# Layer 0 of a two-layer encoder trunk projects the input before its norm is known, and scales the results

## The chip, the cores and the metric

The kernel runs on one core of one Trainium2 chip, as one program. The metric is the device time of one execution in microseconds (us), as the median of several executions. The engines are named as the profile names them: PE is TensorE (matrix products; PEld its weight loads), DVE is VectorE, ACT is ScalarE, POOL is GpSimd, SP is the engine that starts most DMAs.

## The reference

One sequence of 256 tokens, model width 2048, two layers, everything in float32. Per layer (`i`), with `_rmsnorm(x, g)` = x / sqrt(mean(x²) + eps) · g:

```python
hn = _rmsnorm(h, norm_g[i])
u = hn @ w_in[i]
a_val, a_glu, a_z, q, k, v, b_z = jnp.split(u, offs, axis=-1)
ya = _conformer_conv(a_val, a_glu, conv_w[i], conv_b[i], cln_g[i], cln_b[i])
ya = ya * jax.nn.silu(a_z)
...
yb = _window_attention(q, k, v, bias_band, sink[i]) * jax.nn.silu(b_z)
h = h + jnp.concatenate([ya, yb], axis=-1) @ w_out[i]
e = _rmsnorm(p[i] @ w_pe[i], pe_g[i])
h = h + e * jax.nn.sigmoid(h @ w_pg[i])
```

`_conformer_conv` is a·sigmoid(glu), a depthwise convolution of 31 taps along the tokens, a LayerNorm over its 1024 channels, and SiLU. The attention has 16 query heads and 4 key heads of 64, a window of 128 tokens, a relative-position bias and a sink logit per head. `p[i]` is a per-layer embedding of width 256. A final RMSNorm closes the trunk. Since the norm's factor is one number per token, hn @ W is the same as ((h · g) @ W) times that factor of the token.

## The kernel before

Everything lies with channels on the 128 partitions and the 256 tokens along the free axis; a product's result, 128 channels by 256 tokens, is half a PSUM bank, and most results are handled as a bank of two (128x512). A float32 operand is written as a rounded high part (a cast on ACT, type fp32r) and a remainder (a subtraction on DVE); a product of two such operands is three products on PE: high by high, high by remainder, remainder by high (`mm3`, L401 to L403).

The weights stream in "halves" of 512 KB, in the order of the list `HALVES`: 156 per layer. A layer takes them so: 4 of w_pe (the embedding's projection, tile `e`), 32 of `ag` (value and gate columns of the convolution group: the first two tiles together, then one by one), 4 of k, 4 of v, 32 of `zb` (the attention's gate) and q alternating, 16 of `za` (the convolution's gate), 32 of w_out (`o`; first all that goes with `yb`, then all that goes with `ya`), 32 of w_pg (`g`). Each half is loaded into `raw` (pairs of halves, three buffers), cast and subtracted into `w` (five buffers; `split`, L168 and L171), so splits run up to four halves ahead of the products. A half holds 24 products, 3 for each of 8 blocks of 128 channels.

In layer 0 before the change, PE begins with the embedding in plain float32 (L487, 64 passes), while x is loaded, its squares are added (ACT and DVE, the last piece at L495), PE sums them over the partitions into a column per token (`rh0c`, L354), POOL takes the power −1/2 (`rh0col`, L361), and PE makes a row of it that stands on all partitions (`rh0b`, L368). Then DVE makes `hn` = x · gain · row (L455), ACT its high part (L458), DVE the remainder (L459), and the first ag product can run.

The order of work on DVE, PE and ACT is the order in which the program is written (the scheduler is switched off for them). After each half, `pump()` moves side work along: it advances every generator in `side` (attention of each pair of heads, bias, the embedding's norm) by one step, and a queue of convolution taps on DVE (L566, 8 tiles of some 30 instructions per layer) by so many taps as `RATES` says per half. At the last pair of za tiles `finish` runs all taps that are left. Then come the LayerNorm's mean on PE (`mean`, L720, it takes the last taps' tiles) and the products with yb, whose remainders DVE makes there (L755). `embed` squares e tile by tile (ACT), adds the squares (`eacc`, on POOL, L392) during the ag and k halves, and makes the row of the embedding's norm. `rstd_row(..., settle=n)` puts 2n single-column products into PE ahead of the row (L370).

Of the kernel before, what the change touches and what calls it, by code (L numbers as in the profile page):

```python
# [56 lines left out]
NWARM = 6  # L57
QQ = ((4, 5), (2, 4))
# [21 lines left out]
def weight_halves():  # L80
# [7 lines left out]
    for q in range(4):  # L88
        out.append(("w_pe", q, 0, 2))
    for ts in FIRST_TILES:  # L90
        for k0 in (0, 8):
            for t in ts:
                for off in (OFF_VAL, OFF_GLU):
                    out.append(("w_in", off + tile_cols(t), k0, 8))
    for t in range(2):
# [24 lines left out]
HALVES = weight_halves()  # L120
NHALF = len(HALVES)
# [8 lines left out]
def trunk_kernel(ctx: ExitStack, tc: tile.TileContext, xT, pT, wst, par, gain, relb, sinkp, onehot, out):  # L130
# [23 lines left out]
    state = {"raw": -1, "spl": 3, "credit": 0.0}  # L154
    raws, spl = {}, {}
# [7 lines left out]
    def split(h):  # L163
        raw = raws[h // 2][:, h % 2, :]
        w = wspl.tile([P, 2 * HALF + 64], F32R, tag="w", name=f"w{h}")
        w = w[:, SHIFT:SHIFT + 2 * HALF].rearrange("p (t n) -> p t n", t=2)
        hi, lo = w[:, 0], w[:, 1]
        nc.scalar.copy(hi, raw)  # L168
        spl[h] = w
        if h not in (4, 5):  # L170
            nc.vector.tensor_sub(lo, raw, hi.bitcast(F32))  # L171

    def first_lo(h):

        w = spl[h]
        nc.vector.tensor_sub(w[:, 1], raws[h // 2][:, h % 2, :], w[:, 0].bitcast(F32))

    def ahead(h):

        while state["spl"] < min(h, TOT - 1):  # L180
            n = state["spl"] + 1
            while state["raw"] < min(n // 2 + LD - 1, TOT // 2 - 1):
                state["raw"] += 1
                load(state["raw"])
            if HALVES[n % NHALF][0] != "w_pe" or n >= NHALF:
                split(n)
            state["spl"] = n

    def get(h):

        r = h % NHALF
        if r < 12:
# [8 lines left out]
    RATES = (3.3, 2.6, 3.3)  # L201

    def pump(taps=None):
        taps = RATES[(Cursor.h % NHALF > 4 + 32 + 8 + 12) + (Cursor.h % NHALF > 4 + 32 + 8 + 32 + 4)] if taps is None else taps
# [58 lines left out]
    def load_p(l):  # L263
        pf = wk.tile([P, 2, S], F32, name=f"p{l}", tag="v", bufs=1)
        (nc.sync if l == 0 else nc.gpsimd).dma_start(pf, pT[l])
        return pf

    def load_half(c, x, eng=nc.sync, n=1):

        if c not in raws:  # L270
            raws[c] = wraw.tile([P, 2, HALF], F32, tag="raw", name=f"raw{c}")
        w = HALF // n
        for i in range(n):
            eng.dma_start(raws[c][:, x, i * w:(i + 1) * w], wst[c, :, x * HALF + i * w:x * HALF + (i + 1) * w])

    def load_x(k, eng=nc.sync):
        eng.dma_start(h[k // 8][:, k % 8:k % 8 + 4, :], xT[:, k:k + 4, :])

    h = halves(bigt("x"))

    load_half(0, 0, nc.scalar, 2)
    pf = load_p(0)
    load_half(0, 1)
    load_x(0, nc.scalar)
    load_x(4)
    load_half(1, 0, nc.scalar)
    load_x(8)
    load_x(12)
    load_half(1, 1)
    load_half(2, 0)  # L290
    gains = cst.tile([P, (DEPTH + 1) * KT], F32, name="gains")
    nc.sync.dma_start(gains, gain)
    load_half(2, 1)
    state["raw"] = 2
    pars = cst.tile([P, DEPTH * PW], F32, name="pars")
    nc.sync.dma_start(pars, par)
# [52 lines left out]
    def rstd_col(parts, dim, name, idles=0):  # L349

        c = bank(name + "c")
        for x, a in enumerate(parts):
# [3 lines left out]
            if x == 0 and idles:  # L356
                idle(idles)
        v = wk.tile([P, 2], F32, name=name + "v", tag="rv")
        nc.vector.tensor_scalar(v, c[:, 0, 0:2], 1.0 / dim, EPS, ALU.mult, ALU.add)
# [79 lines left out]
    for l in range(DEPTH):  # L439

        e = halves(bigt(f"e{l}"))
        eacc = wk.tile([P, 2, S], F32, name="eacc", tag="hacc")
# [26 lines left out]
        def copied(j, b, e=e):  # L469
            nc.scalar.copy(e[j // 8][:, j % 8:j % 8 + 2, :], b)  # L470

        for q in range(4):
            n = Cursor.h
            Cursor.h += 1
            if l:
                w = get(n).rearrange("p t (j k c) -> p t j k c", j=4, k=2)
            else:
                raw = raws[n // 2][:, n % 2, :].rearrange("p (j k c) -> p j k c", j=4, k=2)
            for jj in range(0, 4, 2):
                j = 4 * q + jj  # L480
                b = bank("e")
                for x in range(2):
                    for k in range(2):
                        if l:
                            mm3(b[:, x, :], w[:, :, jj + x, k, :], pp[:, :, k, :], x == 0 and k == 0, k == 1)
                        else:
                            nc.tensor.matmul(b[:, x, :], raw[:, jj + x, k, :], pf[:, k, :], start=x == 0 and k == 0,  # L487
                                             stop=k == 1, skip_group_check=True)
                if l == 0 and j // 2 < 4:
                    for k in (4 * (j // 2), 4 * (j // 2) + 2):  # L490
                        if k < KT - 2:
                            square_acc(hacc, h[k // 8][:, k % 8:k % 8 + 2, :], k == 0, nc.vector)
                    if j // 2 == 3:
                        sq = wk.tile([P, 2, S], F32, name="sq", tag="sq", bufs=3)
                        nc.scalar.activation(sq, h[1][:, 6:8, :], AF.Square)  # L495
                        hparts = halves_of(sq) + [fold(hacc)]
                if j // 2 == QQ[l][0]:
                    dg = rstd_col(hparts, D, f"rh{l}")
                    ahead(5 if l == 0 else Cursor.h - 1 - q + 5)
                if j // 2 == QQ[l][1]:  # L500
                    rbs.append(rstd_row(dg, f"rh{l}", copy=False))
                    if l == 0:
                        first_lo(4)
                        operands(0, 1)
                        first_lo(5)
                        subs.pop(0)()
                        operands(2, 1)
                if QQ[l][1] + (l == 0) <= j // 2 <= QQ[l][1] + 1:
                    operands(4 * (j // 2 - QQ[l][1]), 2)
                ecopy.append((j, b))  # L510

                while ecopy and 4 * (l == 0) <= j // 2 < 6:
                    copied(*ecopy.pop(0))
            pump()
        subs.pop(0)()
        ahead(Cursor.h + 3)
        for c in ecopy:
            copied(*c)
        hsrc = xT if l == 0 else hscr

        def embed(l=l, eacc=eacc, e=e):

            if l == 0:
                yield from wait(4)
                bias_prep()
# [414 lines left out]
```

## Time and profile before

| | us |
|---|---|
| median of 3 runs | 937.57 (937.34 to 937.88) |
| profiled execution | 938.7 |
| its span | 936.9 |
| PE busy | 923.9 (99%) |
| DVE busy | 767.6 (82%) |
| ACT busy | 549.2 (59%) |
| POOL busy | 82.0 (9%) |

The span is the time from the first to the last instruction of the profiled execution; 1.8 us of that execution lie outside it. Busy times of an engine count its instructions, whether or not anything waits for them. PE's ends are modelled, and consecutive products overlap: a row's length of a product (0.28 us) is more than the distance of two starts. In the timeline's rows stand the start, the length, the engine, the line, the operation and its tiles, the shape, the count, and in brackets the idle time before with what ended it. PEclk is the clock that PE was granted, 1.00 or 0.50 of full speed. Line numbers in rows are those of the kernel before.

### The profile page before, as it was taken

How to read it: one execution, taken by the hardware profiler on the slowest of the kernel's cores; microseconds unless marked ns; L12 is line 12 of the kernel's file. 1: busy time of each engine (PE TensorE's matmuls, PEld its weight loads, DVE VectorE, ACT ScalarE, POOL GpSimd, SP SyncE). 2: the span in 40 equal slices, each digit the busy share in tenths (PEclk: the TensorE clock that was granted, in tenths of full speed). 3: DMA queues.
4: the chain of work that ended last, by engine and by line, in shares of the span. 5: the costliest groups of instructions: out<-in, count | busy, mean ns of one | idle time of the engine just before them, and what ended most of it. 6: DMA issues, size and time to landing. Idle time of an engine off the chain costs nothing.

```text
span 936.9 us, 19106 instructions
## 1 busy us (share of the span) xinstructions
PE 923.9 (99%) x7960; PEld 909.7 (97%) x7960; DVE 767.6 (82%) x1282; ACT 549.2 (59%) x830; POOL 82.0 (9%) x79
## 2 busy tenths in 40 slices
PE   8999999999999999999999999999999999999995
PEld 7999999999999999999999999999999999999995
DVE  3999999998887786787679999999888877777663
ACT  4655454878874555554566445568788546445551
POOL 0013001001000000011102100100100000000111
PEclk9999999999999999999999999999999999999999
DMA  7674656555547455546555556565555554654532
GB/s 298 226 250 150 220 180 230 190 196 175 189 171 247 166 209 212 191 181 230 211 189 193 181 212 226 174 213 196 183 169 180 193 197 152 247 183 179 200 114 91
DMA packets 29011, 182.55 MB, mean 195 GB/s; under 512 B 3595, under 2 KB 4156, under 8 KB 9084
## 3 DMA queue, kind: packets, MB, share of 16 engines
q1 hardware_dynamic: 24284, 165.70, 50.1%
q0 software_dynamic: 3344, 12.88, 4.2%
q10 hardware_dynamic: 1296, 2.75, 0.8%
q8 instruction: 62, 1.02, 0.4%
q14 instruction: 25, 0.20, 0.1%
HBM read 177.09 MB, written 4.23 MB: 194 GB/s over the span
## 4 chain that ended last, share of the span: by engine, by line
PE 75%; DVE 19%; ACT 2%; issue 2%; DMA 1%; ACTq 0%; DVEq 0%
DVE cz L566 8%; DVE w L171 8%; PE o L401 6%; PE o L402 6%; PE o L403 6%; PE g L401 6%; PE g L403 6%; PE g L402 6%; PE ag L403 4%; PE ag L401 4%; PE ag L402 4%; PE za L401 3%; PE za L403 3%; PE za L402 3%; PE av L679 2%
## 5 line engine op out<-in xcount | busy, mean ns | idle before, releaser
L171 DVE TENSOR_TENSOR w<-raw,w 128x1024 fp32r<-128x1024 f32 x306 | 375.1, 1234 | 99.5 <-ACT w L168 98.6
L168 ACT CAST w<-raw 128x1024 fp32r<-128x1024 f32 x308 | 315.6, 1046 | 157.8 <-PE ag L403 42.5
L566 DVE SCALAR_TENSOR_TENSOR cz<-az,pars,cz 128x241 f32<-128x241 f32 (+11 forms) x480 | 215.9, 499 | 1.0
L401 PE MATMUL ag<-hg,w 128*128 128x256 f32 x512 | 141.8, 277 | 0.0
L403 PE MATMUL ag<-hg,w 128*128 128x256 f32 x512 | 141.6, 277 | 0.0
L402 PE MATMUL ag<-hg,w 128*128 128x256 f32 x512 | 141.5, 276 | 0.0
L403 PE MATMUL g<-h,w 128*128 128x256 f32 x512 | 141.3, 276 | 0.0
L401 PE MATMUL g<-h,w 128*128 128x256 f32 x512 | 141.3, 276 | 0.0
L402 PE MATMUL g<-h,w 128*128 128x256 f32 x512 | 141.3, 276 | 0.0
L401 PEld LDWEIGHTS ag<-hg,w 128*128 128x128 f32 x512 | 96.1, 188 | 0.9 <-ACT u L575 0.8
L403 PEld LDWEIGHTS ag<-hg,w 128*128 128x128 f32 x512 | 96.2, 188 | 0.1
L402 PEld LDWEIGHTS ag<-hg,w 128*128 128x128 f32 x512 | 96.1, 188 | 0.0
L401 PEld LDWEIGHTS g<-h,w 128*128 128x128 f32 x512 | 96.1, 188 | 0.0
L402 PEld LDWEIGHTS g<-h,w 128*128 128x128 f32 x512 | 96.1, 188 | 0.0
L403 PEld LDWEIGHTS g<-h,w 128*128 128x128 f32 x512 | 96.1, 188 | 0.0
L401 PE MATMUL za<-hg,w 128*128 128x256 f32 x256 | 71.7, 280 | 0.0
L401 PE MATMUL o<-yb,w 128*128 128x256 f32 x256 | 71.6, 280 | 0.0
L401 PE MATMUL q<-hg,w 128*128 128x256 f32 x256 | 71.5, 279 | 0.0
L401 PE MATMUL zb<-hg,w 128*128 128x256 f32 x256 | 71.5, 279 | 0.0
L402 PE MATMUL o<-yb,w 128*128 128x256 f32 x256 | 71.0, 277 | 0.0
L402 PE MATMUL q<-hg,w 128*128 128x256 f32 x256 | 71.0, 277 | 0.0
L403 PE MATMUL zb<-hg,w 128*128 128x256 f32 x256 | 71.0, 277 | 0.0
(223 smaller groups left out, 2264.4 us busy)
## 6 DMA issues: line engine op xcount, KB each, us to landing
raw<-in_wst SPq DMA_DIRECT2D x153, 1024.0 KB, 4.9
bias<-fscr POOLq DMA_DIRECT2D x16, 384.0 KB, 3.9
raw<-in_wst SPq DMA_DIRECT2D x4, 512.0 KB, 7.9
az<-in_xT POOLq DMA_DIRECT2D x4, 512.0 KB, 6.0
hscr<-e POOLq DMA_DIRECT2D x2, 1024.0 KB, 5.6
az<-hscr POOLq DMA_DIRECT2D x4, 512.0 KB, 5.4
x<-in_xT SPq DMA_DIRECT2D x3, 512.0 KB, 8.2
out_t<-og ACTq DMA_DIRECT2D x4, 256.0 KB, 3.0
```

Of the source, the lines that this page charges most:

```text
L168: nc.scalar.copy(hi, raw)
L171: nc.vector.tensor_sub(lo, raw, hi.bitcast(F32))
L401: nc.tensor.matmul(o, w[:, 0], x[:, 0], start=start, stop=False, skip_group_check=True)
L402: nc.tensor.matmul(o, w[:, 0], x[:, 1], start=False, stop=False, skip_group_check=True)
L403: nc.tensor.matmul(o, w[:, 1], x[:, 0], start=False, stop=stop, skip_group_check=True)
L566: nc.vector.scalar_tensor_tensor(acc[:, t, lo_:hi_], a[:, t, lo_ + s:hi_ + s], w(k), acc[:, t, lo_:hi_], ALU.mult, ALU.add)
L679: nc.tensor.matmul(o[hh * HD:(hh + 1) * HD, x, :], v[:, kt, g * HD:(g + 1) * HD], pt[hh][:, kt, :], start=x == 0 and kt == 0, stop=kt == 1 ...
```

## The change

In layer 0, x is projected without its norm:

- The operands `hg` are gain · x: the high part is made by ACT directly from x, the remainder by DVE, tile by tile (L563, L564 of the changed kernel). The first two ag tiles (halves 0 to 7 of the list) are computed in four groups of 48 products as quarters of the weights (256 KB) and pieces of x land. w_pe stands behind them in the list, and its products are split too: 96 instead of 64 passes.
- The sum of squares comes from a second copy of x with tokens on partitions (a new input `xtok`, 2 MB in eight DMAs): eight squares on ACT that add along the row. POOL takes the root; the row (`rh0rb`, tile `scaled`) is made on PE ahead of the embedding's third quarter, with two settles.
- Each result of layer 0's projections is scaled by that row on DVE as it leaves PSUM (`evicted`, L599 and L601: 21 instructions of 128x512: 8 of ag, 1 of k, 4 each of q, zb and za); v's scale is part of its copy on ACT. ACT reads the scaled tile one or two pumps later (`DELAY`). The queries come before the gates of their pair. Layer 0's first rate of taps is 3.1 instead of 3.3.
- In both layers the embedding's squares move from the ag stage to the second half of w_out, with the adds on DVE instead of POOL, and its row gets settle=2.
- pars, relt, oh and sinkt are loaded later, seven warm-up passes run instead of six, and p of layer 0 comes behind a memset on DVE.

How PE's order at the start stands before (the names: `e` the embedding's result, `p` its input, `rh0c`, `rh0b` the norm):

```order
L261 MATMUL warm<-zeros 128x256 x6
L487 MATMUL e<-p_90,raw_87 128x256 x16
L487 MATMUL e<-p_90,raw_95 128x256 x4
L354 MATMUL rh0c<-ones,sq 128x1 x4
L354 MATMUL rh0c<-ones,fold 128x1 x2
L487 MATMUL e<-p_90,raw_95 128x256 x4
L368 MATMUL rh0b<-ident,rh0col 128x128 x2
L487 MATMUL e<-p_90,raw_95 128x256 x8
L401 MATMUL ag_0_260<-hg_0_214,w_196 128x256
```

And after, the same place:

```order
L266 MATMUL warm<-zeros 128x256 x7
L449 MATMUL ag_0_151<-hg_0_149,w_155 128x256
L450 MATMUL ag_0_151<-hg_0_149,w_155 128x256
L451 MATMUL ag_0_151<-hg_0_149,w_155 128x256
L449 MATMUL ag_0_151<-hg_0_149,w_155 128x256
L450 MATMUL ag_0_151<-hg_0_149,w_155 128x256
L451 MATMUL ag_0_151<-hg_0_149,w_155 128x256
```

The embedding and the norm's products have left the head of PE's list. What ACT has there after the change, in front of those products (three DMAs of weight quarters, then operands' high parts and quarters' casts):

```order
L285 DMA raw_92<-in_wst 128x512 x2
L285 DMA raw_97<-in_wst 128x512
L302 ACT_TABLE_LOAD
L302 ACTIVATE junk<-zeros 128x1
L563 ACTIVATE hg_0_149<-x,gains 128x256
L179 CAST w_155<-raw_92 128x512
L563 ACTIVATE hg_0_149<-x,gains 128x256 x3
L179 CAST w_164<-raw_92 128x512
L179 CAST w_167<-raw_97 128x512
L179 CAST w_170<-raw_97 128x512
```

One operand and one cast stand before the first product, the other three operands and the other quarters behind them. DVE at the end of layer 0's gates, before (taps `cz`, splits `w`, remainders `yb`):

```order
L566 SCALAR_TENSOR_TENSOR cz_258<-az_257,pars,cz_258 128x243
L566 SCALAR_TENSOR_TENSOR cz_258<-az_257,pars,cz_258 128x242
L171 TENSOR_TENSOR w_3494<-raw_3340,w_3494 128x1024
L566 SCALAR_TENSOR_TENSOR cz_258<-az_257,pars,cz_258 128x241
L171 TENSOR_TENSOR w_3522<-raw_3340,w_3522 128x1024
L755 TENSOR_TENSOR yb_3551<-az_257,yb_3551 128x512 x4
```

And after (`ev<-za_6` is the scaling of the last pair of za tiles, `rh0rb` the row):

```order
L180 TENSOR_TENSOR w_3622<-raw_3436,w_3622 128x1024
L622 SCALAR_TENSOR_TENSOR cz_466<-az_465,pars,cz_466 128x245 x2
L622 SCALAR_TENSOR_TENSOR cz_466<-az_465,pars,cz_466 128x244
L599 TENSOR_TENSOR ev<-za_6_3515,rh0rb 128x512
L622 SCALAR_TENSOR_TENSOR cz_466<-az_465,pars,cz_466 128x244
L622 SCALAR_TENSOR_TENSOR cz_466<-az_465,pars,cz_466 128x243
L622 SCALAR_TENSOR_TENSOR cz_466<-az_465,pars,cz_466 128x242
L622 SCALAR_TENSOR_TENSOR cz_466<-az_465,pars,cz_466 128x241
L622 SCALAR_TENSOR_TENSOR cz_466<-az_465,pars,cz_466 128x243
L622 SCALAR_TENSOR_TENSOR cz_466<-az_465,pars,cz_466 128x242
L622 SCALAR_TENSOR_TENSOR cz_466<-az_465,pars,cz_466 128x241
L904 TENSOR_TENSOR yb_3663<-az_465,yb_3663 128x512 x4
```

The scaling of the last za result now stands in front of seven taps, and those in front of yb's remainders. The core of the diff:

```diff
-NWARM = 6
+NWARM = 7
+DELAY = (1, 0)
+O_LAST = 4 + 32 + 4 + 4 + 32 + 16 + NB_FIRST
...
-        for off in (OFF_BZ, OFF_Q):
+        for off in (OFF_BZ, OFF_Q) if l else (OFF_Q, OFF_BZ):
...
-    RATES = (3.3, 2.6, 3.3)
+    RATES = ((3.1, 2.6, 3.3), (3.3, 2.6, 3.3))
...
+            for n in range(4):
+                c = slice((n % 2) * (HALF // 2), (n % 2 + 1) * (HALF // 2))
+                ks = range(4 * n, 4 * n + 4)
+                def part(k):
+                    i, kk = k // 8, k % 8
+                    hi, lo = (x[:, kk, :] for x in halves(hg[i]))
+                    nc.scalar.activation(hi, h[i][:, kk, :], AF.Copy, scale=gcol(l, k))
+                    nc.vector.scalar_tensor_tensor(lo, h[i][:, kk, :], gcol(l, k), hi.bitcast(F32),
+                                                   ALU.mult, ALU.subtract)
+                for y in range(4):
+                    for k in ks[:1] if y == 0 else ks[1:] if y == 1 else []:
+                        part(k)
+                    split_part(4 * (n // 2) + y, c)
+                if n == 1:
+                    small_loads()
+                for y in range(4):
+                    w = spl[4 * (n // 2) + y].rearrange("p t (k c) -> p t k c", k=8)
+                    for k in ks:
+                        mm3(firsts[y // 2][:, y % 2, :], w[:, :, k % 8, :], hg[k // 8][:, :, k % 8, :],
+                            y % 2 == 0 and k == 0, k == KT - 1)
...
+            hilo(pp[:, 0], pp[:, 1], pf)
+            ahead(9)
+            later_loads()
+            for x, y in enumerate(xts):
+                nc.scalar.activation(y, y, AF.Square, accum_out=xs[:, x // 4, x % 4:x % 4 + 1])
...
+            rcol = root(xs[:, :, 0], D, f"rh{l}")
+
+        def evicted(b, scale=None):
+            if scaled is None:
+                return b
+            u = wk.tile([P, 2, S], F32, name="ev", tag="sq", bufs=3)
+            if scale is None:
+                nc.vector.tensor_mul(u, b, bcast2(scaled))
+            else:
+                nc.vector.scalar_tensor_tensor(u, b, scale, bcast2(scaled), ALU.mult, ALU.mult)
+            return u
...
+                if q == 2:
+                    scaled = rstd_row(rcol, f"rh{l}", settle=2)
...
+            while Cursor.h % NHALF < O_LAST:
+                yield
             for j in range(0, KT, 2):
-                yield from wait(2)
-                square_acc(eacc, e[j // 8][:, j % 8:j % 8 + 2, :], j == 0)
+                square_acc(eacc, e[j // 8][:, j % 8:j % 8 + 2, :], j == 0, nc.vector)
+                yield
...
-            eb = rstd_row(dg, f"re{l}", "reb")
+            eb = rstd_row(dg, f"re{l}", "reb", settle=2)
...
-            b = pair(hg, f"za{l}_{t}")
+            b = evicted(pair(hg, f"za{l}_{t}"))
             if t == NCT - 2:
                 finish(l)
...
-                nc.scalar.copy(v[:, b, :], vb[b][:, 0, :])
+                nc.scalar.activation(v[:, b, :], vb[b][:, 0, :], AF.Copy, scale=rcol[:, b:b + 1])
```

More of the change, by code (lines that the diff above doesn't have):

```diff
@@ L86, in std @@
         out.append((name, cols, 8, 8))
-    for q in range(4):
-        out.append(("w_pe", q, 0, 2))
+    if l:
+        out += W_PE
     for ts in FIRST_TILES:
@@ L129, in trunk_kernel @@
 @with_exitstack
-def trunk_kernel(ctx: ExitStack, tc: tile.TileContext, xT, pT, wst, par, gain, relb, sinkp, onehot, out):
+def trunk_kernel(ctx: ExitStack, tc: tile.TileContext, xT, xtok, pT, wst, par, gain, relb, sinkp, onehot, out):
     nc = tc.nc
@@ L264, in load_p @@
         pf = wk.tile([P, 2, S], F32, name=f"p{l}", tag="v", bufs=1)
-        (nc.sync if l == 0 else nc.gpsimd).dma_start(pf, pT[l])
+        nc.gpsimd.dma_start(pf, pT[l])
         return pf
[L268 to L274, printed above, removed]
@@ new lines, in load_x @@
+    def load_x(k, n=4, eng=nc.sync):
+        eng.dma_start(h[k // 8][:, k % 8:k % 8 + n, :], xT[:, k:k + n, :])
+    h = halves(bigt("x"))
+    gains = cst.tile([P, (DEPTH + 1) * KT], F32, name="gains")
+    pars = cst.tile([P, DEPTH * PW], F32, name="pars")
+    pf = wk.tile([P, 2, S], F32, name="p0", tag="v", bufs=1)
+    load_x(0, 2)
+    load_part(0, 0, nc.scalar)
+    nc.sync.dma_start(gains, gain)
+    load_part(1, 0, nc.scalar)
+    load_x(2, 2)
+    load_part(2, 0, nc.scalar)
+    junk = wk.tile([P, 1], F32, name="junk", tag="junk", bufs=1)
@@ L285, in trunk_kernel @@
+    nc.scalar.activation(junk, zeros[:, 0:1], AF.Copy, scale=2.0)
+    load_part(3, 0)
     load_x(4)
-    load_half(1, 0, nc.scalar)
+    for x in range(4):
+        load_part(x, 1)
     load_x(8)
+    for x in range(4, 8):
+        load_part(x, 0)
     load_x(12)
[L289 to L295, printed above, removed]
@@ L296, in trunk_kernel @@
-    nc.sync.dma_start(pars, par)
+    for x in range(4, 8):
+        load_part(x, 1)
+    xts = []
+    for b in range(2):
+        for c in range(4):
+            if b == 0:
+                y = wk.tile([P, 2, S], F32, name="xt", tag="s", bufs=4)
+            elif c < 2:
+                y = wk.tile([P, 2, S], F32, name="xt", tag="ptt", bufs=2)
+            else:
+                y = wk.tile([P, 2, 3 * P], F32, name="xt", tag="bias", bufs=2)
+            y = y.rearrange("p a b -> p (a b)")[:, 0:2 * S]
+            xts.append(y)
@@ L439, in trunk_kernel @@
     for l in range(DEPTH):
-        e = halves(bigt(f"e{l}"))
-        eacc = wk.tile([P, 2, S], F32, name="eacc", tag="hacc")
+        if l:
+            e = halves(bigt(f"e{l}"))
+            eacc = wk.tile([P, 2, S], F32, name="eacc", tag="hacc")
         hg = []
@@ L467, in trunk_kernel, with copied @@
         ecopy = []
-        def copied(j, b, e=e):
+        def copied(j, b):
             nc.scalar.copy(e[j // 8][:, j % 8:j % 8 + 2, :], b)
[L472 to L475, printed above, removed]
-                w = get(n).rearrange("p t (j k c) -> p t j k c", j=4, k=2)
-            else:
[L478 to L514, printed above, removed]
@@ L897, in pack @@
     for l in range(DEPTH):
[L898 removed]
+        for n, (name, cols, k0, nk) in enumerate(HALVES[l * NHALF:(l + 1) * NHALF]):
             w = W[name][l]
```

256 lines of the change are left out of this document (178 added, 78 removed).

## The prediction

> **What bounds the kernel now.** I read the page first, then what TensorE (PE) waits for, then its timeline where it waits, then windows.
>
> ```profile
> span 936.9 us, 19106 instructions
> PE 923.9 (99%) x7960; PEld 909.7 (97%) x7960; DVE 767.6 (82%) x1282; ACT 549.2 (59%) x830; POOL 82.0 (9%) x79
> ```
>
> PE is busy for 99% of the span. Its list of waits (engine, line, releaser: total us, times, longest) names one that this change touches at the start and one in the attention:
>
> ```profile
> PE rh0c L354 <- ACT sq L495: 1.1, 1, 1.1
> PE sc L636 <- DVE qq L696: 0.6, 2, 0.4
> ```
>
> Time is won only where PE idles or works on something dear. That is the start (start, length, work, count):
>
> ```profile
> 5.57 1.99 PE L487 MATMUL e<-p,raw 128*128 128x256 f32 x8
> 8.03 7.17 PE L487 MATMUL e<-p,raw 128*128 128x256 f32 x32 [0.46 <-DMA raw<-in_wst]
> 16.35 1.05 PE L354 MATMUL rh0c<-ones,sq 128*128 128x1 f32 x8 [1.15 <-ACT sq L495]
> 17.71 3.31 PE L487 MATMUL e<-p,raw 128*128 128x256 f32 x8
> 21.24 3.79 PE L487 MATMUL e<-p,raw 128*128 128x256 f32 x16
> 24.69 0.47 PE L401 MATMUL ag<-hg,w 128*128 128x256 f32 x1
> ...
> 42.01 1.03 PE L329 MATMUL fps<-oh,relt 33*16 33x511 f32 x2
> ```
>
> Until 24.69 us PE has only the embedding's 64 fp32 passes, 0.216 us each (the last 16 from 21.24 to 24.69), so 13.8 us of work in 19.1 us. Windows (start:end and length; busy us and count of PE, PEld, DVE, ACT, POOL; then PEclk, DMA share, GB/s; the first row is of the tile ag alone, without POOL):
>
> ```profile
> 24.66:48.50 23.84, 22.93 (x192) 22.58 (x193) 0.40 (x1) 0.38 (x1) 1.00 0.66 230
> ...
> 14.77:18.18 3.41, 2.26 (x16) 1.84 (x16) 2.17 (x6) 2.54 (x4) 0.05 (x1) 1.00 1.12 395
> 18.18:21.59 3.41, 3.41 (x10) 2.67 (x10) 1.11 (x2) 3.25 (x6) 1.57 (x1) 0.50 0.68 263
> ...
> 50.00:190.00 140.00, 139.72 (x1226) 139.31 (x1225) 137.11 (x242) 79.66 (x116) 18.02 (x14) 1.00 0.58 204
> 290.00:460.00 170.00, 170.00 (x1495) 169.84 (x1494) 123.98 (x147) 86.93 (x107) 10.34 (x10) 1.00 0.57 203
> ```
>
> The first two ag tiles (192 products, with fps's 1.03 among them) end at 48.50: (23.84 - 1.03)/192 = 0.1188 us a product. At 18.18 the clock fell to half for a window. In 50 to 190 PE works for 139.72 of 140, and VectorE (DVE) for 137.11: two engines almost full. From 50 on PE hardly has anything to lose or win, so the sum is made of the start and of waits that the change adds.
>
> **The start.** Before, the end of the first two ag tiles is 48.50. After, the work in that stretch is 192 ag products, 96 split embedding products, fps, and a row. Each term:
>
> Embedding: 64 passes of 0.216 = 13.8 become 96 products. A product in the dense stage costs 139.72/1226 = 0.114 us (products of other kinds are among them), so 10.9; gain 2.9. Idle and half clock in the old start, 24.66 - 5.57 - 13.8 = 5.3 us, go, as no product waits for the root any more. What replaces them is the time until the first split operand:
>
> ```profile
> GB/s 0 16 152 244 266 420 422 418 422 414 422 410 410 401 418 380 389 366 369 410 213 16 0 0 147 188 426 336 205 401 311 82 139 401 401 107 0 33 254 410
> raw<-in_wst ACTq DMA_DIRECT2D x2, 256.0 KB, 5.8
> p<-in_pT SPq DMA_DIRECT2D x1, 256.0 KB, 4.6
> L818 ACT ACTIVATE og<-e,gains 128x256 f32<-128x256 f32 x16 | 7.2, 493 | 0.0
> L458 ACT CAST hg<-hn 128x512 fp32r<-128x512 f32 x16 | 9.9, 621 | 13.7 <-DVE hn L455 13.7
> L455 DVE SCALAR_TENSOR_TENSOR hn<-x,gains,rh0b 128x256 f32<-128x256 f32 x16 | 6.7, 473 | 2.3 <-PE rh0b L368 2.3
> L459 DVE TENSOR_TENSOR hg<-hn,hg 128x512 fp32r<-128x512 f32 x16 | 11.0, 688 | 0.5
> ```
>
> The GB/s row is one figure per microsecond from 0; the others are DMAs (KB, us to land) and groups (mean ns last before the idle time). x's first piece and the first weight quarter stand first in their queues, like p and raw here, and land at the same time, about 5.5 (PE's first pass starts at 5.57). Then ACT makes x's hi (0.49) and casts a quarter (0.62): first product at about 6.65, 1.1 later than now. Per group of 48 products ACT has 4 operands and 4 quarters, 4 x 0.49 + 4 x 0.62 = 4.4; DVE 4 x 0.47 + 4 x 0.69 = 4.6; PE 48 x 0.1188 = 5.7. So once fed, PE paces. The first group is not fed: x's second piece and the second to fourth quarters land by about 8 to 9.3 (the GB/s row sums to 1.5 MB by 7 us, what the group needs, plus landing), and DVE must finish each remainder. I take 1.1 us lost; bounds 0 (each piece lands before its turn) and 2.5 (PE waits for the last piece, then works alone). All four groups need 6.3 MB; the row sums to that by 18, the last group starts after 22. Between the embedding's second and third quarter the root's row (2 small products, 4 of settle) costs 0.7:
>
> ```profile
> 20.82 0.63 PE L368 MATMUL rh0b<-ident,rh0col 128*128 128x128 f32 x2
> L391 ACT ACTIVATE sq<-e 128x512 f32<-128x512 f32 x26 | 16.5, 633 | 18.4 <-DVE e L805 18.4
> 18.13 1.63 POOL L361 TENSOR_TENSOR rh0col<-rh0v,mhalf 128x2 f32<-128x2 f32 x1 [16.81 <-DVE rh0v L359]
> ```
>
> Is the root ready by then? First tiles end at 6.65 + 22.8 + 1.1 = 30.6, the third quarter starts at 36.0. ACT starts its eight squares at about 27.3: ahead of them stands the cast of half 9, into the buffer that half 4's last products leave at 26.3 (5 buffers). 8 x 0.63 = 5.1, two small adds, POOL's 1.63: 34.4. Ready, by 1.6 us; if it were later, each 1 us would cost 1.
>
> So −2.9 − 5.3 + 1.1 + 1.1 + 0.7 = **−5.3 us**: half 12 starts at 43.2, not 48.5.
>
> **A new wait at the end of layer 0's gates.** Here the order of DVE is what counts. Before:
>
> ```profile
> 289.01 0.46 DVE L566 SCALAR_TENSOR_TENSOR cz<-az,pars,cz 128x241 f32<-128x241 f32 x1
> ...
> 291.92 0.28 PE L403 MATMUL za<-hg,w 128*128 128x256 f32 x1
> 292.04 0.59 PE L720 MATMUL mean<-ysum,ones 128*128 128x256 f32 x2
> 292.47 1.03 PE L720 MATMUL mean<-cz,ones 128*128 128x256 f32 x4
> 293.15 0.47 PE L401 MATMUL o<-yb,w 128*128 128x256 f32 x1
> ```
>
> The last tap ended 2.5 us ahead of the last za product; mean follows it without a gap, o starts 1.2 later. After, with 0.2 taps fewer per pump for some 44 pumps, about 9 taps come later: seven stand behind `ev<-za_6`, which waits for that same last product. Behind it on DVE: the scaling (0.60 at pitch, 0.69 alone by the L768 row), seven taps, then yb's remainders, which o needs. From Z, the last product's start: 0.3 for its end, 0.6, seven taps of 0.39 (pitch, from 1.26 for three below) = 2.7: last tap at Z + 3.7, its mean pass until about Z + 4.2, and o behind it. That is **+3.0** against Z + 1.2 (bounds 2.7 and 3.3, by one tap either way). PE idles some 2.8 us of it, in two pieces. Layer 1's order there stays.
>
> **Scalings on DVE.** 21 scalings at the L768 row's pitch, 0.60, are 12.6 us, ten of them in 50 to 190, 6.0 us where DVE has 2.9 free. Against them: 44 x 0.2 taps of 0.39 moved later, 3.4, and POOL's seven adds of squares leave, which slow DVE:
>
> ```profile
> L768 DVE TENSOR_TENSOR az<-o,az 128x512 f32<-128x512 f32 x16 | 10.9, 684 | 0.7 <-PE o L403 0.6
> 77.65 2.23 POOL L392 TENSOR_TENSOR eacc<-eacc,sq 128x512 f32<-128x512 f32 x1 [3.77 <-ACT sq L391]
> 78.65 2.29 DVE L566 SCALAR_TENSOR_TENSOR cz<-az,pars,cz 128x250 f32<-128x250 f32 x3
> 82.00 1.26 DVE L566 SCALAR_TENSOR_TENSOR cz<-az,pars,cz 128x255 f32<-128x255 f32 x3
> ```
>
> Three taps take 2.29 beside a POOL add and 1.26 without: 7 x 1.03 = 7.2 us back. DVE ends lighter by 4.6: the scalings cost 0. The scaled result is read a pump later by ACT, and DVE never waits for ACT there. The same squares now stand in w_out, eight adds of 0.69 on DVE per layer, where DVE has 170 - 124 = 46 us free: 0. There the cover is so large that even doubled they are hidden. xtok's 2 MB go in a stretch (20 to 40) where the GB/s row is mostly below 200: 0. The later loads (pars and the rest) are needed first by the taps and the bias products, after 43: 0.
>
> **Small terms.** Settle: four 128x1 products ahead of a row,
>
> ```profile
> 313.63 0.50 PE L370 MATMUL rv0b<-ones 128*128 128x1 f32 x4
> 314.00 0.36 PE L401 MATMUL o<-yb,w 128*128 128x256 f32 x1
> ```
>
> 0.37 by the distance of the starts, now before two rows more (the embedding's root, both layers): +0.7. The 0.6 us of sc's wait for q's remainders: in layer 0 a whole pair of gates now stands between q and the next q, in both layers DVE is relieved of POOL's adds; I take −0.5, bounds −0.6 and 0. One moved term counts nothing: v is scaled by ACT instead of copied, same length.
>
> **Sum.** −5.3 + 3.0 + 0.7 − 0.5 = −2.1. The profiled execution took 938.7, its span 936.9, the median of the runs 937.57, so it was 1.1 above; after's profile should read 936.6 with a span of 934.8, and the median **935.5**. A difference of 0.2%, 1.9 us (935.7 to 939.4 is "same"), is about what can be told from no change.
>
> **Rivals.**
>
> The finish drops the clock. The 14.77 window above had 12 thin products and four passes, 0.86 of real work, and the next window ran at 0.50, which costs half of 3.41, 1.7 us. In the tail PE kept its clock:
>
> ```profile
> 926.12:929.53 3.41, 1.71 (x13) 1.28 (x12) 2.00 (x5) 0.37 (x1) 1.88 (x2) 1.00 0.15 51
> 929.53:932.95 3.42, 0.00 (x0) 0.00 (x0) 1.90 (x4) 0.00 (x0) 1.32 (x2) 1.00 0.99 361
> 932.95:936.90 3.95, 0.00 (x0) 0.00 (x0) 0.00 (x0) 0.00 (x0) 0.00 (x0) 0.50 0.47 176
> ```
>
> 1.71 of busy time was enough; so the threshold lies between. The finish has 2.8 idle around six mean passes (1.3): a window placed worst holds 0.9 to 1.3 of work. Then 935.5 + 1.7 = 937.2, "same". I give it 0.18.
> The Trainium skill, page "TensorE: Matmul & The Clock Gate", section "Why this matters for your kernels", says a drop needs a gap in the products of over about 3 us. By that rule a gap of 2.8 us in two pieces keeps the clock, this rival has no chance and the sum stays 935.5; the trace doesn't bear it out, since the clock fell after 1.15 us of idle and thin products.
>
> The start is fed late: the bound of 2.5 instead of 1.1 lost, or a window at half clock after the thin warm-up: 935.5 + 1.4 to 1.7, about 937. For it: two engines and two queues must follow each other for the first group; against it: the queues deliver 420 GB/s by 5 us. 0.10.
>
> The start goes better: no loss in the first group (−1.1) and the 192 products at the later 0.114 instead of 0.1188 (−1.0), as no bias products and splits of whole halves stand beside them: 933.4. 0.16.
>
> The other side: the scalings are not covered. If POOL's adds were not what slowed the taps (the three taps beside them may have been slow for ACT's sake), DVE has 6.0 - 2.9 - 3.4 against it, nearly nothing, so this needs more: a scaling waits for its PE result, and all taps and splits behind it wait with it. At 0.6 us of such wait for each of ten, 6 us, PE waits for the remainders: 941.5. It is slower than 939.4 from 3.9 us uncovered. Against it: the splits run up to four halves, 11 us, ahead of PE. 0.08.
>
> **How the numbers follow.** The sum as it stands has 0.48, its own range 934.0 to 936.8 (start 1 us, finish 0.3). Faster: 0.31 of that, and the better start, 0.16: 0.47. Slower: 0.08. Same: the rest, 0.45. The range, 932.8 to 938.3, takes in the better start, the half-clock cases and the sum with all bounds, and leaves out the uncovered scalings and the ends.
>
> **What would show it.** Right: the first product at 6.4 to 7, half 12 near 43.2; a gap of about 2 us on PE behind za_6, put down to DVE cz; no wait of PE for w in 50 to 190; taps without the 2.29 rows there; sc's wait gone. Wrong: PE waits for DVE w in 50 to 190, or PEclk 0.50 behind 285, or half 12 later than 45.

## The result

The changed kernel takes 951.74 us (median of 5, 950.97 to 952.49) against 937.34 before: ratio 1.0152, 95% interval 1.0137 to 1.0167. It is slower by 14.4 us, where 2 us faster was forecast. The profiled execution took 950.98, with this head of its page:

```profile
span 949.2 us, 19291 instructions
PE 933.4 (98%) x7994; PEld 920.2 (97%) x7994; DVE 771.3 (81%) x1322; ACT 558.5 (59%) x861; POOL 58.2 (6%) x65
```

The span grew by 12.3. Marks on PE, read from the two timelines, say where (us; L0 and L1 are layer 0 and 1; "step" is what the difference gained or lost against the mark above):

| mark | before | after | after − before | step |
|---|---|---|---|---|
| third ag tile starts (before: behind fps; after: fps's 0.96 added) | 48.50 | 43.3 | −5.2 | −5.2 |
| L0, last ag product ends | 113.97 | 109.29 | −4.7 | +0.5 |
| L0, last za product ends | 292.20 | 286.37 | −5.8 | −1.1 |
| L0, first o | 293.15 | 291.72 | −1.4 | +4.4 |
| L0, first g | 382.10 | 386.02 | +3.9 | +5.3 |
| L1, last za product ends | 746.04 | 749.85 | +3.8 | −0.1 |
| L1, first g | 836.41 | 845.70 | +9.3 | +5.5 |
| L1, last g ends | 923.62 | 936.31 | +12.7 | +3.4 |
| end of span | 936.9 | 949.2 | +12.3 | −0.4 |

The start gave what it was to give, and a little more followed until the end of the za products: 5.8 us ahead. The four steps of +3.4 to +5.5 behind it lose 18.6. The list of PE's waits names two of their causes:

```profile
PE mean L869 <- DVE cz L622: 3.0, 2, 2.9
PE re1c L398 <- DVE fold L427: 1.9, 1, 1.9
```

**The end of layer 0's gates** (timeline of after, PE, then DVE):

```profile
286.21 0.59 PE L869 MATMUL mean<-ysum,ones 128*128 128x256 f32 x2
289.66 1.22 PE L869 MATMUL mean<-cz,ones 128*128 128x256 f32 x2 [2.86 <-DVE cz L622]
291.06 1.22 PE L869 MATMUL mean<-cz,ones 128*128 128x256 f32 x2 [0.17 <-DVE cz L622]
...
284.73 1.23 DVE L180 TENSOR_TENSOR w<-raw,w 128x1024 fp32r<-128x1024 f32 x1
285.87 1.24 DVE L622 SCALAR_TENSOR_TENSOR cz<-az,pars,cz 128x245 f32<-128x245 f32 x3
287.02 0.69 DVE L599 TENSOR_TENSOR ev<-za,rh0rb 128x512 f32<-128x512 f32 x1
287.62 3.38 DVE L622 SCALAR_TENSOR_TENSOR cz<-az,pars,cz 128x244 f32<-128x244 f32 x7
290.92 2.49 DVE L904 TENSOR_TENSOR yb<-az,yb 128x512 fp32r<-128x512 f32 x4
```

The seven taps stand there as forecast, but the scaling starts at 287.02, 0.6 after za's end: a split and three more late taps are ahead of it. The seven taps also take longer than forecast, 3.30 from the first one's start to that of yb's remainders instead of 2.7: five of them start 0.50 apart, two 0.39. The mean waits 2.86, and its last four passes take 1.22 a pair instead of 0.6.

**The clock** (windows of after: length; busy us and count of PE, PEld, DVE, ACT, POOL; PEclk, DMA share, GB/s):

```profile
285.65:289.07 3.42, 1.15 (x9) 0.75 (x7) 3.35 (x8) 1.33 (x3) 0.00 (x0) 1.00 0.63 184
289.07:292.48 3.41, 2.64 (x6) 1.75 (x7) 3.30 (x8) 1.01 (x3) 0.55 (x1) 0.50 0.29 123
292.48:295.89 3.41, 3.41 (x18) 3.41 (x17) 3.15 (x5) 1.51 (x3) 1.06 (x2) 0.50 0.85 283
821.55:824.96 3.41, 1.67 (x14) 1.70 (x15) 2.19 (x4) 1.18 (x2) 0.00 (x0) 1.00 0.30 58
824.96:828.38 3.42, 3.42 (x18) 3.42 (x17) 3.00 (x5) 1.33 (x2) 1.06 (x1) 0.50 0.59 249
```

Twice a window in which PE was busy for 1.15 and 1.67 of 3.41 us is followed by half clock. The first drop lasts two windows; in the first of these PE was busy for 2.64. All five executions of after have a mean granted clock of 0.992 or 0.993, so these drops are not of the profiled one alone.

**A slow rhythm of PE**, which the prediction did not know. Windows over the 768 products of w_pg (tile g alone, so PE, PEld, ACT), called the last gates in layer 1; first layer 1 before, then both layers after:

```profile
836.41:923.62 87.21, 87.21 (x768) 87.01 (x768) 4.58 (x8) 1.00 0.42 146
```

```profile
386.02:473.22 87.20, 87.20 (x768) 87.00 (x768) 4.58 (x8) 1.00 0.58 206
845.70:936.31 90.61, 90.61 (x768) 90.41 (x768) 4.58 (x8) 1.00 0.40 140
```

The same 768 products, no wait, PEclk 1.00 throughout: 87.2/768 = 0.1135 us each in layer 0 and before, 90.6/768 = 0.1180 in layer 1. From product to product the starts stand 0.1133 or 0.1178 us apart, and one of the two holds for tens of us. Summing what products at 0.1178 take over 0.1133 (without those of the embedding), this rhythm costs 3.4 us in the execution before and 10.2 in the one after: 2.2 in layer 0's w_out, 3.4 in layer 1's g.

So L0's w_out pays about 2.1 for half clock (4.17 us of o until 295.89), 2.1 for slow rhythm (0.1 of it stood there before), 1.4 for the column products and row of the embedding's norm (0.7 each, by the distance of the starts of the o products around them); L1's w_out 1.95 for the wait, 1.6 for half clock, 1.4 for column and row, 0.6 for slow rhythm; L1's g 3.4 for slow rhythm.

### The profile page after: what moved, and what is told of

Its sections match the earlier page's. It is cut to its first block, busy times and chain, and to the rows that moved or that the text cites. A ratio compares the mean times of both kernels' runs of the same rounds, so it can differ in the third digit from the quotient of the medians.

```text
span 949.2 us, 19291 instructions
## 1 busy us (share of the span) xinstructions
PE 933.4 (98%) x7994; PEld 920.2 (97%) x7994; DVE 771.3 (81%) x1322; ACT 558.5 (59%) x861; POOL 58.2 (6%) x65
## 4 chain that ended last, share of the span: by engine, by line
PE 95%; DVE 2%; issue 1%; DMA 1%; ACT 1%; SPq 0%; DVEq 0%; ACTq 0%
PE g L449 6%; PE g L451 6%; PE g L450 6%; PE ag L451 6%; PE ag L450 6%; PE ag L449 6%; PE o L449 6%; PE o L450 6%; PE o L451 6%; PE zb L450 3%; PE zb L449 3%; PE q L450 3%; PE q L449 3%; PE zb L451 3%; PE q L451 3%; PE za L449 3%
## 5 line engine op out<-in xcount | busy, mean ns | idle before, releaser
L180 DVE TENSOR_TENSOR w<-raw,w 128x1024 fp32r<-128x1024 f32 (+1 forms) x316 | 378.5, 1206 | 118.7 <-ACT w L179 117.5
L179 ACT CAST w<-raw 128x1024 fp32r<-128x1024 f32 (+1 forms) x316 | 319.7, 1029 | 175.1 <-PE ag L451 31.1
L622 DVE SCALAR_TENSOR_TENSOR cz<-az,pars,cz 128x241 f32<-128x241 f32 (+14 forms) x480 | 203.5, 476 | 1.2 <-ACT cz L615 0.3
L449 PE MATMUL o<-yb,w 128*128 128x256 f32 x256 | 73.0, 285 | 0.0
L449 PE MATMUL o<-ya,w 128*128 128x256 f32 x256 | 72.3, 283 | 0.0
L450 PE MATMUL o<-yb,w 128*128 128x256 f32 x256 | 72.2, 282 | 0.0
L451 PE MATMUL o<-yb,w 128*128 128x256 f32 x256 | 72.1, 282 | 0.0
L450 PE MATMUL o<-ya,w 128*128 128x256 f32 x256 | 72.0, 281 | 0.0
L451 PE MATMUL o<-ya,w 128*128 128x256 f32 x256 | 71.9, 281 | 0.0
```

The lines of the kernel that those rows point to most:

```text
L449: nc.tensor.matmul(o, w[:, 0], x[:, 0], start=start, stop=False, skip_group_check=True)
L450: nc.tensor.matmul(o, w[:, 0], x[:, 1], start=False, stop=False, skip_group_check=True)
L451: nc.tensor.matmul(o, w[:, 1], x[:, 0], start=False, stop=stop, skip_group_check=True)
L622: nc.vector.scalar_tensor_tensor(acc[:, t, lo_:hi_], a[:, t, lo_ + s:hi_ + s], w(k), acc[:, t, lo_:hi_], ALU.mult, ALU.add)
```

## The experiments

Theories: **A**, late taps and a late fold make PE wait, and the clock drops behind the waits. **B**, DVE simply has no room for the scalings. **C**, an interruption of PE's stream of big products sets its rhythm until the next one. First, A's parts:

```diff
# e1_rate33 (from after)
-    RATES = ((3.1, 2.6, 3.3), (3.3, 2.6, 3.3))
+    RATES = ((3.3, 2.6, 3.3), (3.3, 2.6, 3.3))
# e2_fold3 (from after); e3_both is both
             es = fold(eacc)
-            yield
+            yield from wait(3)
# e4_fill (from after), between mean's ysum pass and its last two tiles
+                if x == 1 and l == 0:
+                    idle(12)
```

> The changed kernel with layer 0's first rate of taps at 3.3 per half, as before the change. Theory A (the loss at the end of layer 0's gates is late taps: seven behind the last scaling and three ahead of it, and two windows at half clock that the idle PE brings): no tap is left behind the last scaling, mean follows za without a long gap, o starts about 1.5 us after the last za product instead of 5.6, no window at half clock there: 951.7 - 4.1 - 2.1 = 945.5; up to 2 less if the slow rhythm of PE in w_out behind it (0.1178 us a product instead of 0.1133) goes too. Theory B (DVE is simply overloaded by the 21 scalings, the rate only moves where it shows): PE waits for DVE w between 50 and 190, by about the same 3 to 4 us, and the time stays within 1 us of 951.7.

946.95 (median of 4, 945.69 to 951.54), ratio to before 1.0115 [1.0088, 1.0142]. No wait but one of 0.3 for yb and no half clock is left at the finish, PE's rows (timeline of e1) are those of before, and o starts 1.0 after za's end:

```profile
287.90 0.59 PE L869 MATMUL mean<-ysum,ones 128*128 128x256 f32 x2
288.33 1.03 PE L869 MATMUL mean<-cz,ones 128*128 128x256 f32 x4
289.01 0.47 PE L449 MATMUL o<-yb,w 128*128 128x256 f32 x1
```

But za now ends at 288.06 instead of 286.37. Its list of waits has a new one:

```profile
PE pt L787 <- ACT s L781: 1.3, 2, 0.9
```

A holds for the finish. B as forecast fell, since the time dropped by 4.8 and PE waits for weights for no more than 0.2, but DVE's load has a share: 1.7 us come back ahead of the finish, 1.3 of them as this wait of the attention.

> The changed kernel with three pumps instead of one between the fold of the embedding's squares and the column products that need it, both layers. Theory A (PE waits 1.9 us for a fold that DVE makes one half of weights too late; idle time and thin products drop the clock for a window): the wait, the window at 825 and so 1.9 + 1.7 us go, 951.7 - 3.6 = 948.1. Theory C (the slow rhythm of PE in the last 100 us, 0.1178 instead of 0.1133, comes from how PE was interrupted there): another 4.0 us go if the rhythm changes with it, 944; if the rhythm is of something else (DVE's or ACT's load), it stays slow and 948.1 holds.

947.12 (943.77 to 947.91), 1.0096 [1.0073, 1.0118]. The wait for the fold is gone, and so is the half clock at 825. The last gates stay slow in the profiled run (90.6 us), so the forecast of 948 holds. 943.77, the lowest of the four, is about what 0.1133 a product there would give; that execution was not profiled.

> Rate 3.3 in layer 0's first stage and three pumps behind the fold together. Theory A: the two add up, 951.7 - 6.2 - 3.6 = 941.9, still over before; with the slow rhythm gone from both w_out stages and the last gates (2.2 + 4.0) 935.7. Theory B: no better than the fold alone, 947 to 948.

943.54 (939.94 to 943.65), 1.0060 [1.0040, 1.0080]: the two nearly add up (−4.8 and −4.6, together −8.2). Three runs lie at 943.5 to 943.65 and one at 939.94; the profile, of that one, has the last gates fast (87.2 us). The mean granted clock of all four is 0.997 or 0.998, so the 3.6 between them is not the clock; it is about what one slow stretch of 768 products costs. The same kernel seems to run either way, though only the one at 939.94 was profiled.

> The changed kernel with twelve products of no use (128x128, some 0.22 us each, 2.6 us in all) on PE between mean's pass over ysum and its passes over the last two tiles, in layer 0: PE is busy while it would wait for the late taps. Theory A: the wait stays, the clock doesn't drop there: 951.7 - 2.1 (o at half clock) - 0.6 (mean's four passes) = 949.0, windows at 285 to 296 all at 1.00. If the clock goes by something else than PE's idle time, 951.7 and windows at 0.50.

948.9 (946.6 to 951.25), 1.0127 [1.0106, 1.0148]. Two windows of it at the bounds of those of after, and the rows of PE:

```profile
285.65:289.07 3.42, 3.42 (x31) 3.37 (x29) 3.31 (x9) 1.54 (x3) 0.00 (x0) 1.00 0.59 213
289.07:292.48 3.41, 2.53 (x15) 1.83 (x15) 3.34 (x7) 1.54 (x4) 0.74 (x2) 1.00 0.22 94
```

```profile
286.43 2.84 PE L391 MATMUL idle<-ident,ones 128*128 128x128 f32 x24
289.46 0.70 PE L871 MATMUL mean<-cz,ones 128*128 128x256 f32 x2 [0.18 <-DVE cz L622]
290.85 0.70 PE L871 MATMUL mean<-cz,ones 128*128 128x256 f32 x2 [0.69 <-DVE cz L622]
```

o starts 0.5 earlier than in after (291.20), so the wait is the taps', but o's first products no longer run at half clock: by the time of the first ya product layer 0 is 2.4 ahead of after. With PE's idle time filled, the clock stayed. The drop at 825 is missing in this profile too, as in that of e1, though both wait 1.9 to 2.0 for the fold like after. In e1 that idle time falls on two windows:

```profile
815.49:818.90 3.41, 2.21 (x20) 2.02 (x18) 3.29 (x4) 1.56 (x3) 0.00 (x0) 1.00 0.42 175
818.90:822.31 3.41, 2.65 (x23) 2.68 (x24) 1.77 (x4) 2.16 (x3) 0.00 (x0) 1.00 0.57 199
```

Neither is as idle as the 1.67 of after, and the clock stays. In e4 the clock's windows lie so that most of the idle time falls in one:

```profile
816.87:820.28 3.41, 1.78 (x16) 1.58 (x14) 3.41 (x5) 1.11 (x2) 0.00 (x0) 1.00 0.25 103
```

PE was busy for 1.78 here, none of it single-column products, and kept its clock; the 1.67 of after has four of those in it (0.58). So whether this wait costs the clock hangs on where it falls in a window. Three of e1's four executions and two of e4's have a mean granted clock of 0.995 where the profiled ones have 0.997; one window more at half clock would make 0.0018, so the drop probably came back in those. The median of e4 is 2.8 lower than after's.

Next, the squares' place, the settle, and the taps:

```diff
# e5_oldemb (from e3): embed of before; squares in ag and k, adds on POOL, row in the attention, no settle
# e6_settle0, e8_settle4 (from e3)
-            eb = rstd_row(dg, f"re{l}", "reb", settle=2)
+            eb = rstd_row(dg, f"re{l}", "reb")            # e8: settle=4
# e7_rates (from e3)
-    RATES = ((3.3, 2.6, 3.3), (3.3, 2.6, 3.3))
+    RATES = ((3.1, 2.9, 3.6), (3.3, 2.6, 3.3))
```

> Rate 3.3 and the embedding's squares, fold, column and row back in the ag and k stages and the attention, adds on POOL, no settle, as before the change (the start unnormed and the scalings stay). Theory C (an interruption of PE's stream sets its rhythm, 0.1133 or 0.1178 us a product, until the next one; the row of the embedding's norm is the last one ahead of 840 products of layer 1): the last one is now the LayerNorm's row, behind which all profiles so far that had no slow w_out before it were fast: the last gates run at 0.1133, 3.4 less than the 943.5 of the version with both repairs, 1.6 less for the column products and rows that leave w_out: 938.5, and up to 1.5 less in layer 0's w_out. Theory B (DVE has no room in ag for scalings beside POOL's adds, so the move of the squares was needed): PE waits for w or for the attention's results by 2 to 7 us more: 941 to 945.

952.03 (948.4 to 956.22), 1.0155 [1.0114, 1.0195], 8.5 worse than e3. Its list of waits:

```profile
PE q L451 <- DVE w L180: 3.8, 2, 3.2
PE pt L788 <- ACT s L782: 2.1, 2, 1.7
```

B is right for this version: with POOL's adds beside the scalings DVE falls behind, PE waits for weights, the clock drops at 141.5, and nearly all later stretches run slow (16 us in the profile). So at these rates of taps moving the squares was needed to pay for the scalings. Those waits are the smaller part, though: of the 15.0 us between the profiled executions of e5 and e3 the slow rhythm makes about 10, and the two waits above 4.6 more than e3's. Theory C's forecast that the last gates would be fast here fell: behind the LayerNorm's row they were slow.

> Both repairs (rate 3.3, three pumps behind the fold), with no settle products ahead of the embedding's row. Theory C (rhythm redrawn by each interruption, its outcome depends on the timing of the pieces): the last gates are fast or slow as a whole, for this kernel mostly one way; 943.5 - 0.7 = 942.8 if slow, 939.4 if fast. Rival (settle products guard against the slow rhythm): slow more often, 942.8 in all runs.

943.47 (942.77 to 947.29), 1.0070. In the profile layer 0's g products are slow (90.6), layer 1's fast: without settle products each layer came out its own way, which neither forecast has.

> Both repairs, but the taps made up for in layer 0's later stages: rates 3.1, 2.9, 3.6 instead of 3.3, 2.6, 3.3. Theory A': with 3.3 in ag and q, DVE fell behind and the transposes waited 1.3 us for ACT at the attention's start, where the changed kernel had no such wait; with 3.1 there and DVE's 10 us of free time from 188 to 284 used for the taps, that wait goes: za ends 1 to 1.7 earlier, 943.5 - 1.3 = 942.2. Rival: the wait comes back in later pairs: 943.5.

938.95 (median of 10), 1.0021 [1.0008, 1.0033]; two of the ten at 942.7, the others at 938.5 to 939.4. The attention's wait is gone and za ends at 286.69. DVE had room for the late taps, in the later stages. The median lies 3.2 under the forecast because the last gates are mostly fast here, by the times of the ten, and were mostly slow in e3; against e3's execution of 939.94 the gain is 1.0.

> Both repairs, with eight single-column products of settle instead of four ahead of the embedding's row. Theory C: the row takes 0.45 longer in each layer, and the rhythm behind it is drawn anew: 944.4 if the last gates are slow, 941.0 if fast. Rival (more settle makes the fast rhythm sure): 941.0 in all runs.

941.52 (940.84 to 943.56), 1.0047. Last gates fast in the profile. Behind the row of layer 1, settle 4 was fast and settle 2 came out either way: more products are no guard by themselves, since in e7, by their times, eight runs of ten are fast with 2.

Then theory C alone, on the kernel before, and a version with all waits repaired:

```diff
# e11_draw2, e12_draw1 (from before), between layer 1's w_out and its gates; 2 or 1
+        if last:
+            for x in range(2):
+                nc.tensor.matmul(bank("draw")[:, 1, 0:1], ones, ones[:, 0:1], start=True, stop=True)
# e9_best (from e7): the last scaling behind yb's remainders; two pumps from fold to column, three to the row
-            b = evicted(pair(hg, f"za{l}_{t}"))
+            b = pair(hg, f"za{l}_{t}")
+            if t < NCT - 2:
+                b = evicted(b)
...
+        begin(rest(evicted(b), 0))
         lgen = lnorm()
# e10_best0: e9 with no settle in the embedding's rows
```

> The kernel before the change, with two single-column products (four passes) between layer 1's w_out and its gates, nothing else. Theory C: an interruption alone redraws the rhythm for the last 768 products: 937.5 + 0.4 = 937.9 in the runs that come out fast, 941.3 in those that come out slow, and at least one of each or all slow. Rival (the slow rhythm comes from the changed kernel's load of DVE or its memory layout, not from the interruption): 937.9 in all runs and pitch 0.1133 in the profile.

> The kernel before the change with one single-column product (two passes) at that place. Theory C: as with two, 937.7 or 941.1. Rival: 937.7 in all runs.

With two products 940.54 (all of six runs 940.3 to 941.9), 1.0036 [1.0022, 1.0049]; with one 937.33 (twelve runs, none over 938.6), 1.0001 [0.9992, 1.0009]. Windows over the g tile of layer 1, of e11 and of e12:

```profile
834.74:925.44 90.70, 90.70 (x768) 90.49 (x768) 4.57 (x8) 1.00 0.40 140
```

```profile
835.14:922.43 87.29, 87.29 (x768) 87.09 (x768) 4.58 (x8) 1.00 0.41 145
```

That is C with nothing else of the change: two products of no use, 0.4 us, put the following 768 into the slow rhythm, 3.4 us; one does not. It isn't drawn by lot here: by their times, all runs with the same count have the rhythm of the one that was profiled. One rival is left in this pair: each of these products takes a PSUM bank of its own, so with two of them the g tiles lie one bank further on than with one. The runs e9 and e14 below settle it: there the extra products share the row's bank.

> The version with the rates 3.1, 2.9, 3.6, and the rest of the losses repaired: the last scaling behind yb's remainders instead of ahead of them (o waits 0.6 less for yb), two pumps between fold and column and three between column and row instead of three and two (the 0.4 to 0.5 that PE waits for POOL's root in layer 1 goes). Theory A: 938.9 - 0.6 - 0.5 = 937.8 with the last gates at the fast rhythm, 941.2 with the slow one. Rival (the waits come back elsewhere): 938.9.

941.24 (six runs, 940.84 to 941.97), 1.0040 [1.0028, 1.0052]: no wait of PE over 0.4 us is left behind the start, but the last gates are slow:

```profile
836.74:927.36 90.62, 90.62 (x768) 90.41 (x768) 4.57 (x8) 1.00 0.41 146
```

> The same without settle in the embedding's rows. Theory C: 937.8 - 0.7 = 937.1 if both stretches of gates are fast, 3.4 more for each that is slow. Rival (the settle products make the fast rhythm likely): slow in one of the two in nearly all runs, 940.5.

944.56 (944.05 to 945.12), 1.0075 [1.0062, 1.0088]: both layers' g products slow. So the count was varied once more, in e9:

```diff
# e13_re1: settle=1; e14_re21: settle=2 - l; e15_re23: settle=2 + l
-            eb = rstd_row(dg, f"re{l}", "reb", settle=2)
+            eb = rstd_row(dg, f"re{l}", "reb", settle=1)
# e16_all1: settle=2 - l there, and
-            rb = rstd_row(dg, f"rv{l}", settle=2)
+            rb = rstd_row(dg, f"rv{l}", settle=1)
```

> The repaired version (941.2) with settle 1 instead of 2 in the embedding's rows of both layers. Theory C (the rhythm behind an interruption depends on how many products it has; one single-column product in the kernel before left it fast, two left it slow): 0.4 less in all, and layer 1's gates fast: 941.2 - 0.4 - 3.4 = 937.4, or 3.4 more if layer 0's gates, fast so far, become slow. Rival (something else of the change costs the 3.9): 940.8.

> The repaired version with settle 2 in layer 0's embedding row (fast behind it so far) and 1 in layer 1's (slow behind 2). Theory C: 941.2 - 0.2 - 3.4 = 937.6. Rival: 941.0.

> The repaired version with settle 2 in layer 0 and 3 in layer 1. Theory C, if an odd number is what matters: 941.2 + 0.2 - 3.4 = 938.0; if only a small number helps: 941.4. Rival: 941.4.

> The repaired version with settle 2 and 1 in the embedding's rows and 1 instead of 2 in the LayerNorm's rows of both layers, behind which layer 0's w_out ran slow (1.4 us). Theory C: 941.2 - 0.2 - 3.4 - 0.4 - 1.4 = 935.8 if all stretches come out fast, 1.4 more if layer 0's w_out stays slow. Rival: 940.6.

936.83, 937.14 and 938.11 for e13 to e15 (ratios 1.0002, 1.0006, 1.0012; eleven runs each): the last gates are fast behind 1 and 3, as in this window of e14, and nothing is left of the 3.9. The forecasts were 937.4, 937.6 and 938.0. Then e16, forecast at 935.8, **934.49** (nine runs, 934.21 to 935.72), 0.9975 [0.9966, 0.9985]: with layer 0's w_out fast for nearly all of its length as well (0.55 us of slow rhythm against 2.9 in e14) it beats both kernels, the one before by 0.25%. Between e9 and e14 only the number of products in layer 1's row differs, in the same bank. Windows of e14 and e16, and e16's waits:

```profile
835.59:922.80 87.21, 87.21 (x768) 87.01 (x768) 4.58 (x8) 1.00 0.42 154
```

```profile
833.86:921.07 87.21, 87.21 (x768) 87.00 (x768) 4.58 (x8) 1.00 0.43 154
```

```profile
PE warm L266 <- DVE zeros L263: 1.2, 1, 1.2
PE rfc L398 <- ACT sq L963: 0.4, 1, 0.4
PE ag L451 <- DVE w L180: 0.2, 1, 0.2
```

## Why the prediction was wrong

**The start: right.** Forecast −5.3 with half 12 at 43.2, measured −5.2 at 43.3. That it fits so well is partly luck, since three misses cancel: the first product runs at 6.98 (6.65), the first two ag tiles take 23.2 (23.9) as their products run at 0.113 and not 0.1188, and the embedding with its row takes 12.2 (11.6). The path was as forecast: the root's power ends at 33.7 (34.4), the row's products start at 35.94 (36.0):

```profile
6.98 0.38 PE L449 MATMUL ag<-hg,w 128*128 128x256 f32 x1 [0.26 <-ACT w L179]
...
32.97 0.70 POOL L409 TENSOR_TENSOR rh0col<-rh0v,mhalf 128x2 f32<-128x2 f32 x1 [31.66 <-DVE rh0v L407]
...
35.94 0.38 PE L416 MATMUL rh0b<-ident,rh0col 128*128 128x128 f32 x2
```

**The finish: right mechanism, size missed.** +3.0 was forecast within 2.7 to 3.3, +4.4 measured. The step that failed took the scaling to start 0.3 after za's last product; it started 0.6 later than that, behind a split and three late taps, which the order of DVE shows ahead of it and the sum left out. The seven taps behind it were priced at 0.39 each, a distance taken from taps at 82 us, and took 0.6 more in all; in the trace of before, taps from 286 on already start 0.50 to 0.51 apart. Why the distance differs isn't shown. The half clock did the rest, 0.2, on mean's passes.

**The clock: a rival at 0.18, and it happened.** Its price was one window; it was two, and a second drop came at 825 where none was looked for. The bound "1.71 of busy time was enough", from the tail, was taken for a threshold; the window 821.55 dropped with 1.67, single-column products among them. Busy time alone is no threshold: the window 14.77 of before dropped with 2.26, most of it such products, and e4's kept its clock with 1.78. The rule of the Trainium skill, page "TensorE: Matmul & The Clock Gate", section "Why this matters for your kernels", asks for a gap over about 3 us; here a longest gap of 2.86 and one of 1.95 dropped it, so the measurement decides against that figure. Gaps of 1.95 in e1 and 1.94 in e4 did not, so no single length of gap decides either.

**Settle and the embedding's move: the worst step.** "Eight adds ... per layer, where DVE has 46 us free: 0" (seven in the trace) priced how much DVE works, not what waits for it. Before, three pumps lay between the fold and the column products; after, one, and DVE's order puts a split ahead of the fold. In layer 1 (DVE's rows):

```profile
821.59 1.22 DVE L180 TENSOR_TENSOR w<-raw,w 128x1024 fp32r<-128x1024 f32 x1
822.73 0.42 DVE L427 TENSOR_TENSOR fold<-eacc 128x256 f32<-128x256 f32 x1
```

PE, whose last o product before this started at 821.06, waited 1.95, and the clock took 1.6. In layer 0, where PE had been slower, the same order cost no wait. Also the column and the row were moved into w_out, not only given settle: 1.4 a layer there instead of 0.37, most of it a cost that left an earlier stage.

**The rhythm: absent, and the largest term.** 6.8 of the 12.3 us. Both rhythms stood in the trace of before (products 0.1133 and 0.1178 apart, 3.4 us in all); the prediction averaged them to 0.114 and read 0.1188 at the start as a matter of the stage. What changed for layer 1's g: the last interruption ahead of it was the LayerNorm's row, and became the embedding's row. That the details of this row decide is shown by e9, e14 and e15; the place alone does not, since e5 has the old place back and ran slow.

An interruption is not the only thing that switches the rhythm. In after, the v products end and the q products begin without a gap or another product between (windows of PE; 96 products start in each):

```profile
120.01:130.89 10.88, 10.88 (x98) 1.00 0.48 171
130.89:142.20 11.31, 11.31 (x98) 1.00 0.38 135
```

That is 0.1133 and 0.1178 a product. The v products have the places of the two operands exchanged. The same switch stands at the end of v in both layers of every changed kernel but e5; before, and in layer 1 of e5, the embedding's column products stand at that border, and the rhythm behind them stays fast. So moving the column away let the slow rhythm in there too, for 29 us of layer 0 (1.1 us); summed to the end of za it is 0.3 more than before in layer 0 and 0.8 in layer 1.

**The balance.** The span was forecast 2.1 shorter and became 12.3 longer. Of these 14.4 us the rhythm makes 6.8, half clock 3.7, the wait for the fold 1.95 and the finish 1.4; 0.5 is left, the net of small terms.

**The scalings: 0, as forecast, as long as the squares' adds leave POOL** (window of after):

```profile
50.00:190.00 140.00, 140.00 (x1217) 139.02 (x1217) 135.63 (x255) 76.55 (x109) 8.82 (x9) 1.00 0.60 211
```

PE is busy for all of it. e5 shows the same scalings with POOL's adds and a rate of 3.3: PE waits 3.8 us for weights. Small terms: −0.5 for sc's wait, −1.1 measured to the end of za, where the embedding's row has left too.

## What to carry to other kernels

Follow each moved wait to what is queued ahead of its releaser on a busy in-order engine; a stage with time to spare does not make a result ready in time. Count what stands ahead of the waited-for instruction, not only behind it. Where products run back to back for long, measure the distance of their starts in each stretch, and after each interruption and each change of operands anew.

## What the runs showed of the hardware

PE runs the same fp32r products at 0.1133 or 0.1178 us apart, at PEclk 1.00 both. Within a stretch of like products with nothing between them the rhythm held in the profiles, once over 768 products and more (3.4 us); it changed behind interruptions by other products, and, without one, at the end of the v products (in both layers of 14 profiles). The count of single-column products in an interruption decides in some places (2 slow, 1 fast in e11 and e12; 0 and 2 slow, 1 and 3 fast in layer 1 of e10, e9, e13 to e15), and elsewhere executions of one kernel seem to differ (e3, e7). Behind layer 0's row 2 was fast where in layer 1 it was slow, so the count alone isn't the rule; what in the engine sets it stays open. Windows of 3.41 us with PE busy for 1.15, for 1.67 and, mostly with single-column products, for 2.26 were followed by half clock; others with 1.71 and 1.78 were not. One window with 2.64 at half clock did not end it.
